# One DMA queue or two: loads from SyncE, stores from ScalarE, and other chunk sizes, in a softmax with a relative position bias

## The chip, the cores and the metric

The kernel runs on one core of a Trainium2 chip. Data lies in HBM, the large memory; the engines work on SBUF, a memory of 128 partitions (rows) on the core. DMA engines, 16 for the core, move data between the two. A transfer is issued by an engine's instruction queue (here that of SyncE, called SP, or that of ScalarE, called ACT), and the DMA engines then carry it out on their own. VectorE (DVE) and ScalarE compute; TensorE is not used.

The metric is the device time of one execution in microseconds (us). Before the change three runs gave 1330.45, 1329.27 and 1329.56, so the median is 1329.56 us.

## The reference

```python
B, H, S = (2, 8, 2112);  max_rel = 16
rel  = pos[:, None] - pos[None, :]
bias = rel_bias[:, np.clip(rel, -16, 16) + 16]          # (H, S, S)
logits = logits + bias[None]
logits = logits - logits.max(axis=-1, keepdims=True)
exp = np.exp(logits)
return exp / exp.sum(axis=-1, keepdims=True)
```

The input `logits` has 2 x 8 x 2112 x 2112 float32 values, 285.5 MB, and the output has as many. Each row of 2112 values gets a bias that depends only on the distance from the diagonal (33 different values per head), and then a softmax. Every value is read once and written once.

## The kernel before, in words

**Tiling.** Heads are taken in pairs, `K = H // 2 = 4` of them, and for each pair both batches, so there are 8 head pairs of matrices. The 128 partitions are 2 heads x 64 blocks, and a block is `W = 33` consecutive rows of a matrix. So partition p holds 33 rows of one head, contiguous in HBM. These 33 rows are cut into chunks: `SIZES = [6, 5, 6, 5, 6, 5]` (L35). A chunk of r rows is one transfer of 128 partitions x r rows x 8448 bytes, and it lies in one of `NBUF = 4` buffers `X[b]`, b = m % 4. `CH` (L39) lists the `NT = 12` chunks of one value of k (two batches of six), and a loop over k runs four times, so there are 48 chunks in all.

**The bias.** At the start of each k, `strip(k)` (L143) builds on VectorE a strip `F` of 2112 + 32 values per partition, such that the bias of row i of any block is a window of `F`, shifted by one for each row.

**A chunk's work.** `add(m)` (L169, VectorE) waits for the load, then for each row adds the bias, writes the negated sum and its minimum (L173). `exps(m)` (L178, ScalarE) follows row by row: the exponential and its sum (L181). `scale(m)` (L186, VectorE) waits for all of the chunk's exponentials, takes the reciprocals of the sums (L189), and multiplies the first `DV = 3` rows (L193); `scale_rest(m)` (L195) multiplies the other 2 or 3 rows on ScalarE (L198). VectorE starts on the next chunk's `add` only after its part of the scaling, so the chunks are computed one after the other.

**Order of transfers.** All loads and stores are issued by SyncE, on one queue (q1 of the profile), which is worked off in the order of issue. `load` (L86) issues the load of a chunk. `store` (L90) first waits for the scaled rows of VectorE (`scaled`) and of ScalarE (`scaledA`). The first four loads come first, then store 0, and then `turn` (L214) repeats: store chunk n, wait until store n - 1 has landed (its buffer is free), load chunk n + 3 into that buffer. The last chunk's store is cut in two, the 3 rows of VectorE and the 2 of ScalarE (L227, L228). `take(eng, sem, n)` (L82) is a wait for a semaphore to reach n, followed by taking n off it; each engine's loop over k (L202, L207, L221) is a real loop, so the counts must return to their start within a turn.

Of the kernel before, what the change touches and what calls it, by code (L numbers as in the profile page):

```python
# [11 lines left out]
ENG = mybir.EngineType  # L12
# [3 lines left out]
def kernel(  # L16
# [6 lines left out]
    nc = tc.nc  # L23
    P = 128
    B, H, S, S2 = logits.shape
    assert S == S2
    MR = 16
    W = 2 * MR + 1
    NB = S // W
    K = H // 2  # L30
# [1 line left out]
    FW = S + W - 1  # L32
    BIG = 3.0e38
    NBUF = 4
    SIZES = [6, 5, 6, 5, 6, 5]  # L35
    R = max(SIZES)
    assert sum(SIZES) == W

    CH = [(b, sum(SIZES[:i]), r) for b in range(B) for i, r in enumerate(SIZES)]  # L39
    NT = len(CH)  # L40
    assert NT % NBUF == 0

    io = ctx.enter_context(tc.tile_pool(name="io", bufs=1))
    X = [io.tile([P, R * S], FP32, tag=f"X{b}", name=f"X{b}") for b in range(NBUF)]
# [5 lines left out]
    tot = io.tile([P, NBUF * R], FP32, tag="tot", name="tot")  # L50
    rec = io.tile([P, NBUF * R], FP32, tag="rec", name="rec")
# [7 lines left out]
    def rows(t, k, m, s0, n):  # L59

        b, j, r = CH[m]
        return bass.AP(
            tensor=t.tensor,
            offset=t.offset + (b * H * S + j + s0) * S + k * (2 * S * S),
            ap=[[W * S, P], [1, n * S]],
        )

    with tc.tile_critical(no_gpsimd_drain=True):  # L68
        ld = [nc.alloc_semaphore(f"ld{b}") for b in range(NBUF)]
        st = [nc.alloc_semaphore(f"st{b}") for b in range(NBUF)]  # L70
        added = nc.alloc_semaphore("added")
        expd = nc.alloc_semaphore("expd")
        scaled = nc.alloc_semaphore("scaled")
        scaledA = nc.alloc_semaphore("scaledA")
        inv = nc.alloc_semaphore("inv")
        invA = nc.alloc_semaphore("invA")
        rb = nc.alloc_semaphore("rb")
        zero = nc.alloc_semaphore("zero")
        idx = nc.alloc_semaphore("idx")
        dve = nc.alloc_semaphore("dve")  # L80

        def take(eng, sem, n):  # L82
            eng.wait_ge(sem, n).then_inc(sem, -n)  # L83


        def load(k, m):  # L86
            b, r = m % NBUF, CH[m][2]
            nc.sync.dma_start(out=X[b][:, 0 : r * S], in_=rows(logits, k, m, 0, r)).then_inc(ld[b], 16)

        def store(k, m, s0=0, n=None):  # L90
            b, n = m % NBUF, n or CH[m][2]
            if s0 < DV:
                take(nc.sync, scaled, DV)
            if s0 + n > DV:
                take(nc.sync, scaledA, s0 + n - DV)
            nc.sync.dma_start(
                out=rows(out, k, m, s0, n), in_=X[b][:, s0 * S : (s0 + n) * S]
            ).then_inc(st[b], 16)

        for m in range(NBUF):  # L100
            load(0, m)

        Q = 32
        step = list(F.ap[0])[0]
        nc.vector.memset(F[:, 0 : H * W], 0.0).then_inc(zero, 1)  # L105
        nc.scalar.wait_ge(zero, 1)
        nc.scalar.dma_start(
            out=bass.AP(tensor=F.tensor, offset=F.offset, ap=[[Q * step, P // Q], [1, H * W]]),
            in_=bass.AP(tensor=rel_bias.tensor, offset=rel_bias.offset, ap=[[0, P // Q], [1, H * W]]),
        ).then_inc(rb, 16)  # L110
        for p0 in (0, NB):
            nc.gpsimd.iota(  # L112
                F[p0 : p0 + NB, H * W : H * W + NB], pattern=[[-1, NB]], base=0,
                channel_multiplier=1, allow_small_or_imprecise_dtypes=True,
            ).then_inc(idx, 1)

        v = nc.vector
        done = [0]

        def then(ins):  # L120
            done[0] += 1
            ins.then_inc(dve, 1)

        def settle():
            take(v, dve, done[0])
            done[0] = 0


        v.wait_ge(idx, 2)
        iq = F[:, H * W : H * W + NB]  # L130
        for m, op in ((eq, ALU.is_equal), (lt, ALU.is_gt), (gt, ALU.is_lt)):
            then(v.tensor_scalar(out=m, in0=iq, scalar1=0.0, scalar2=None, op0=op))  # L132
        v.wait_ge(rb, 16)
        then(v.stream_shuffle(out=F[:, 0 : H * W], in_=F[:, 0 : H * W], mask=[0] * Q))  # L134
        settle()
        for h in range(2):
            p = slice(h * NB, (h + 1) * NB)
            src = bass.AP(tensor=F.tensor, offset=F[p].offset + h * W,
                          ap=[[list(F.ap[0])[0], NB], [2 * W, K], [1, W]])
            then(v.tensor_copy(out=rbP[p], in_=src))  # L140
        settle()

        def strip(k):  # L143

            then(v.tensor_copy(out=rbK[:, :], in_=rbP[:, bass.ds(k, 1), :]))  # L145
            settle()
            low, high = rbK[:, W - 1 : W], rbK[:, 0:1]
            blocks = view(F, MR, [[W, NB], [1, W]])
            then(v.tensor_tensor(out=blocks, in0=view(eq, 0, [[1, NB], [0, W]]),  # L149
                                 in1=view(rbK, W - 1, [[0, NB], [-1, W]]), op=ALU.mult))  # L150
            then(v.tensor_scalar(out=rest, in0=lt, scalar1=low, scalar2=None, op0=ALU.mult))  # L151
            then(v.tensor_copy(out=F[:, 0:MR], in_=low.to_broadcast([P, MR])))  # L152
            then(v.tensor_copy(out=F[:, FW - MR : FW], in_=high.to_broadcast([P, MR])))  # L153
            settle()
            then(v.scalar_tensor_tensor(out=rest, in0=gt, scalar=high, in1=rest, op0=ALU.mult, op1=ALU.add))  # L155
            settle()
            then(v.tensor_tensor(out=blocks, in0=blocks, in1=view(rest, 0, [[1, NB], [0, W]]), op=ALU.add))  # L157
            settle()

        def row(m, i):  # L160
            return X[m % NBUF][:, i * S : (i + 1) * S]

        def col(t, m, i, n=1):
            c = m % NBUF * R + i
            return t[:, c : c + n]

        DV = 3

        def add(m):  # L169
            take(v, ld[m % NBUF], 16)  # L170
            j, r = CH[m][1:]
            for i in range(r):
                v.tensor_tensor_reduce(  # L173
                    out=row(m, i), in0=row(m, i), in1=F[:, W - 1 - j - i : W - 1 - j - i + S],
                    scale=-1.0, scalar=BIG, op0=ALU.add, op1=ALU.min, accum_out=col(nmax, m, i),
                ).then_inc(added, 1)

        def exps(m):  # L178
            for i in range(CH[m][2]):
                take(nc.scalar, added, 1)  # L180
                nc.scalar.activation(  # L181
                    out=row(m, i), in_=row(m, i), func=ACTF.Exp, scale=-1.0, bias=col(nmax, m, i),
                    accum_out=col(tot, m, i),
                ).then_inc(expd, 1)

        def scale(m):  # L186
            r = CH[m][2]
            take(v, expd, r)
            v.reciprocal(out=col(rec, m, 0, r), in_=col(tot, m, 0, r)).then_inc(inv, 1)  # L189
            v.wait_ge(inv, 1).then_inc(inv, -1)  # L190
            v.sem_inc(invA, 1)
            for i in range(DV):
                v.tensor_scalar_mul(out=row(m, i), in0=row(m, i), scalar1=col(rec, m, i)).then_inc(scaled, 1)  # L193

        def scale_rest(m):  # L195
            take(nc.scalar, invA, 1)
            for i in range(DV, CH[m][2]):
                nc.scalar.activation(  # L198
                    out=row(m, i), in_=row(m, i), func=ACTF.Copy, scale=col(rec, m, i),
                ).then_inc(scaledA, 1)  # L200

        with nc.Fori(0, K, 1, engines=[ENG.DVE]) as k:  # L202
            strip(k)
            for m in range(NT):
                add(m)
                scale(m)
        with nc.Fori(0, K, 1, engines=[ENG.Activation]):  # L207
            for m in range(NT):
                exps(m)
                scale_rest(m)  # L210

        def turn(k, first, stop):  # L214
            for n in range(first, stop):
                store(k + n // NT, n % NT)
                take(nc.sync, st[(n - 1) % NBUF], 16)
                load(k + (n + 3) // NT, (n + 3) % NT)

        store(0, 0)  # L220
        with nc.Fori(0, K - 1, 1, engines=[ENG.SP]) as k:  # L221
            turn(k, 1, NT + 1)
        turn(K - 1, 1, NT - 3)
        for m in range(NT - 3, NT - 1):
            store(K - 1, m)
        r = CH[NT - 1][2]
        store(K - 1, NT - 1, 0, DV)  # L227
        store(K - 1, NT - 1, DV, r - DV)  # L228
        for b in range(NBUF):
            take(nc.sync, st[b], 32 if b == (NT - 1) % NBUF else 16)  # L230


# [28 lines left out]
```

## Time and profile before

| what | value |
|---|---|
| median of the runs | 1329.56 us |
| profiled execution, its own time | 1329.3 us |
| its span (first to last recorded work) | 1327.5 us |
| VectorE busy | 819.7 us, 62% |
| ScalarE busy | 808.8 us, 61% |
| bytes read and written | 285.48 MB and 285.47 MB |
| rate over the span | 430 GB/s |
| the queue q1, share of the 16 DMA engines' time | 99.8% |

The span is what the profile records of the execution; 1.8 us of the profiled execution's own time lie outside it. The rate counts loads and stores together. A queue's share of 16 engines is the time that its packets took, summed, over 16 times the span. "SPq", "ACTq" and "DVEq" in the profile's rows are the instruction queues of SyncE, ScalarE and VectorE: a row that names one as the releaser tells that the wait instruction at that line held the engine. What such a wait waited for is read from the code; for `add` it is the load of the chunk.

### The profile page before, as it was taken

The page shows a single profiled execution, that of the slowest core. Times are in us where ns is not written, and L with a number is a line of the kernel's source. Part 1 is how long each engine was busy: PE and PEld are TensorE (multiplying, and loading weights), DVE is VectorE, ACT ScalarE, POOL GpSimd, SP SyncE. Part 2 cuts the span into 40 slices and gives each one's busy share as a digit, 9 for nine tenths or more (in the row PEclk, how much of TensorE's full clock was granted, in tenths as well). Part 3 has the DMA queues.
Part 4 walks back from the last instruction along what each step waited for, and adds up shares of the span by engine and source line. Part 5 has one row for each costly group of instructions (what it writes and reads, how often), then busy time and mean ns, then how long its engine had stood idle before and what let it go on. Part 6 is the DMA issues. An engine that isn't in the chain of part 4 may idle for free. (4 is left out here: it accounts for less than half of the span.)

```text
span 1327.5 us, 2383 instructions
## 1 busy us (share of the span) xinstructions
DVE 819.7 (62%) x756; ACT 808.8 (61%) x652; POOL 0.6 (0%) x6
## 2 busy tenths in 40 slices
DVE  6875665558655566556866466664686547665572
ACT  3885575655756557555676566764667646675472
POOL 0000000000000000000000000000000000000000
DMA  9999999999999999999999999999999999999998
GB/s 407 427 424 425 430 433 429 432 431 433 434 430 438 423 439 431 432 432 433 438 436 429 433 430 435 433 430 441 427 439 428 435 431 437 434 436 427 436 427 376
DMA packets 13981, 571.00 MB, mean 430 GB/s; under 512 B 1556, under 2 KB 1560, under 8 KB 1560
## 3 DMA queue, kind: packets, MB, share of 16 engines
q1 hardware_dynamic: 13968, 570.96, 99.8%
q14 instruction: 5, 0.04, 0.0%
q10 hardware_dynamic: 8, 0.00, 0.0%
HBM read 285.48 MB, written 285.47 MB: 430 GB/s over the span
## 5 line engine op out<-in xcount | busy, mean ns | idle before, releaser
L173 DVE CUSTOM_DVE_ANT_0 X<-X,F 128x2112 f32<-128x2112 f32 x264 | 605.5, 2354 | 346.8 <-DVEq L83 346.8
L181 ACT ACTIVATE X<-X,nmax 128x2112 f32<-128x2112 f32 x264 | 542.2, 2054 | 411.5 <-ACTq L83 385.7
L198 ACT ACTIVATE X<-X,rec 128x2112 f32<-128x2112 f32 x120 | 238.7, 2046 | 29.0 <-ACTq L83 29.0
L193 DVE TENSOR_SCALAR X<-X,rec 128x2112 f32<-128x2112 f32 x144 | 181.4, 1316 | 11.6 <-DVEq L190 11.6
L189 DVE RECIPROCAL rec<-tot 128x6 f32<-128x6 f32 (+1 forms) x48 | 9.1, 190 | 116.1 <-DVEq L83 116.1
L181 ACT ACTIVATION_READ_ACCUMULATOR X<-X,nmax 128x1 f32 x264 | 49.3, 187 | 0.0
L181 ACT ACT_TABLE_LOAD x4 | 5.1, 1283 | 55.8 <-ACTq L83 55.8
L173 DVE DVE_READ_ACCUMULATOR2_ANT nmax<- 128x1 f32 x264 | 21.7, 82 | 0.0
L157 DVE TENSOR_TENSOR F<-F,rest 128x2112 f32<-128x2112 f32 x4 | 9.4, 2358 | 0.6
L149 DVE TENSOR_TENSOR F<-Z,rbK 128x2112 f32<-128x2112 f32 x4 | 9.4, 2358 | 0.6
L134 DVE LOAD_MASK_SELECT F<-F x1 | 0.0, 14 | 7.1 <-DMA F<-in_rel_bias_dram 7.1
L155 DVE SCALAR_TENSOR_TENSOR rest<-Z,rbK,rest 128x64 f32<-128x64 f32 x4 | 1.1, 284 | 0.6 <-DVEq L83 0.2
L151 DVE TENSOR_SCALAR rest<-Z,rbK 128x64 f32<-128x64 f32 x4 | 1.1, 275 | 0.0
L105 DVE MEMSET F<- 128x264 f32 x1 | 0.3, 278 | 1.1 <-SPq L68 1.1
L145 DVE COPY rbK<-rbP 128x33 f32 x4 | 0.7, 178 | 0.3 <-DVEq L83 0.3
L153 DVE COPY F<-rbK 128x16 f32<-128x16 f32 x4 | 0.7, 168 | 0.0
L152 DVE COPY F<-rbK 128x16 f32<-128x16 f32 x4 | 0.7, 166 | 0.0
L132 DVE TENSOR_SCALAR Z<-F 128x64 f32<-128x64 f32 x3 | 0.5, 223 | 0.1
L140 DVE COPY rbP<-F 64x132 f32<-64x132 f32 x2 | 0.4, 224 | 0.2
L134 DVE STREAM_SHUFFLE F<-F 128x264 f32<-128x264 f32 x1 | 0.4, 443 | 0.0
L112 POOL IOTA F<- 64x64 f32 x2 | 0.4, 179 | 0.7 <-PEq L256 0.6
L245 POOL MEMSET const-bfloat16-1.0<- 128x1 bf16 x1 | 0.1, 103 | 0.0
(3 smaller groups left out, 0.3 us busy)
## 6 DMA issues: line engine op xcount, KB each, us to landing
X<-in_logits_dram SPq DMA_DIRECT2D x24, 6336.0 KB, 39.7
out_dram<-X SPq DMA_DIRECT2D x24, 6336.0 KB, 46.9
X<-in_logits_dram SPq DMA_DIRECT2D x24, 5280.0 KB, 42.2
out_dram<-X SPq DMA_DIRECT2D x23, 5280.0 KB, 48.6
out_dram<-X SPq DMA_DIRECT2D x1, 3168.0 KB, 16.5
out_dram<-X SPq DMA_DIRECT2D x1, 2112.0 KB, 21.1
F<-in_rel_bias_dram ACTq DMA_DIRECT2D x1, 4.1 KB
```

The lines of the kernel that those rows point to most:

```text
L145: then(v.tensor_copy(out=rbK[:, :], in_=rbP[:, bass.ds(k, 1), :]))
L149: then(v.tensor_tensor(out=blocks, in0=view(eq, 0, [[1, NB], [0, W]]), in1=view(rbK, W - 1, [[0, NB], [-1, W]]), op=ALU.mult))
L151: then(v.tensor_scalar(out=rest, in0=lt, scalar1=low, scalar2=None, op0=ALU.mult))
L152: then(v.tensor_copy(out=F[:, 0:MR], in_=low.to_broadcast([P, MR])))
L153: then(v.tensor_copy(out=F[:, FW - MR : FW], in_=high.to_broadcast([P, MR])))
L155: then(v.scalar_tensor_tensor(out=rest, in0=gt, scalar=high, in1=rest, op0=ALU.mult, op1=ALU.add))
L157: then(v.tensor_tensor(out=blocks, in0=blocks, in1=view(rest, 0, [[1, NB], [0, W]]), op=ALU.add))
L173: v.tensor_tensor_reduce(out=row(m, i), in0=row(m, i), in1=F[:, W - 1 - j - i : W - 1 - j - i + S], scale=-1.0, scalar=BIG, op0=ALU.add, o ...
L181: nc.scalar.activation(out=row(m, i), in_=row(m, i), func=ACTF.Exp, scale=-1.0, bias=col(nmax, m, i), accum_out=col(tot, m, i),).then_inc( ...
L189: v.reciprocal(out=col(rec, m, 0, r), in_=col(tot, m, 0, r)).then_inc(inv, 1)
L193: v.tensor_scalar_mul(out=row(m, i), in0=row(m, i), scalar1=col(rec, m, i)).then_inc(scaled, 1)
L198: nc.scalar.activation(out=row(m, i), in_=row(m, i), func=ACTF.Copy, scale=col(rec, m, i),).then_inc(scaledA, 1)
```

## The change

Four edits go together.

1. **Two queues.** `store` is now issued by ScalarE, at the end of each chunk's `scale_rest` in ScalarE's loop. SyncE issues the loads alone: `turn` waits for store n to land and then loads chunk n + 4 into the same buffer.
2. **Chunk sizes.** The first batch of a head pair is cut into 3, 6, 6, 6, 6, 6 rows and the second into 6, 6, 6, 6, 5, 4. There are still 12 chunks for each k and 48 in all. The last store is one transfer of 4 rows.
3. **Division of the scaling.** VectorE takes `r // 2` rows of a chunk of r (3 of 6, 2 of 5, 2 of 4, 1 of 3), ScalarE the rest. Before, VectorE took 3 always.
4. **Waits.** `scaledA` and `invA` are gone: both engines count on `scaled`, and both wait for a running count of `inv` that is put back at the last chunk of a turn. `exps` waits for `added` to reach i + 1 and takes the whole count off at the last row, instead of one at each row.

```diff
-    SIZES = [6, 5, 6, 5, 6, 5]
-    R = max(SIZES)
+    SIZES = [[3, 6, 6, 6, 6, 6], [6, 6, 6, 6, 5, 4]]
+    R = 6
...
-        def store(k, m, s0=0, n=None):
-            b, n = m % NBUF, n or CH[m][2]
-            if s0 < DV:
-                take(nc.sync, scaled, DV)
-            if s0 + n > DV:
-                take(nc.sync, scaledA, s0 + n - DV)
-            nc.sync.dma_start(
-                out=rows(out, k, m, s0, n), in_=X[b][:, s0 * S : (s0 + n) * S]
-            ).then_inc(st[b], 16)
+        def dv(m):
+            return CH[m][2] // 2
+
+        def store(k, m):
+            b, r = m % NBUF, CH[m][2]
+            take(nc.scalar, scaled, r)
+            nc.scalar.dma_start(out=rows(out, k, m, 0, r), in_=X[b][:, 0 : r * S]).then_inc(st[b], 16)
...
         def exps(m):
-            for i in range(CH[m][2]):
-                take(nc.scalar, added, 1)
+            r = CH[m][2]
+            for i in range(r):
+                if i < r - 1:
+                    nc.scalar.wait_ge(added, i + 1)
+                else:
+                    take(nc.scalar, added, r)
...
+        def scales_begin(eng, m):
+            if m < NT - 1:
+                eng.wait_ge(inv, m + 1)
+            else:
+                take(eng, inv, NT)
+
         def scale(m):
             r = CH[m][2]
             take(v, expd, r)
-            v.reciprocal(out=col(rec, m, 0, r), in_=col(tot, m, 0, r)).then_inc(inv, 1)
-            v.wait_ge(inv, 1).then_inc(inv, -1)
-            v.sem_inc(invA, 1)
-            for i in range(DV):
+            v.reciprocal(out=col(rec, m, 0, r), in_=col(tot, m, 0, r)).then_inc(inv, 1 if m < NT - 1 else NT + 1)
+            scales_begin(v, m)
+            for i in range(dv(m)):
...
         def scale_rest(m):
-            take(nc.scalar, invA, 1)
-            for i in range(DV, CH[m][2]):
+            scales_begin(nc.scalar, m)
+            for i in range(dv(m), CH[m][2]):
                 nc.scalar.activation(
                     out=row(m, i), in_=row(m, i), func=ACTF.Copy, scale=col(rec, m, i),
-                ).then_inc(scaledA, 1)
+                ).then_inc(scaled, 1)
...
             for m in range(NT):
                 exps(m)
                 scale_rest(m)
+                store(k, m)
...
         def turn(k, first, stop):
             for n in range(first, stop):
-                store(k + n // NT, n % NT)
-                take(nc.sync, st[(n - 1) % NBUF], 16)
-                load(k + (n + 3) // NT, (n + 3) % NT)
-
-        store(0, 0)
+                take(nc.sync, st[n % NBUF], 16)
+                load(k + (n + NBUF) // NT, (n + NBUF) % NT)
+
         with nc.Fori(0, K - 1, 1, engines=[ENG.SP]) as k:
-            turn(k, 1, NT + 1)
-        turn(K - 1, 1, NT - 3)
-        for m in range(NT - 3, NT - 1):
-            store(K - 1, m)
-        r = CH[NT - 1][2]
-        store(K - 1, NT - 1, 0, DV)
-        store(K - 1, NT - 1, DV, r - DV)
...
+            turn(k, 0, NT)
+        turn(K - 1, 0, NT - NBUF)
+        for m in range(NT - NBUF, NT):
+            take(nc.sync, st[m % NBUF], 16)
```

More of the change, by code (lines that the diff above doesn't have):

```diff
@@ L34 @@
     NBUF = 4
-    SIZES = [6, 5, 6, 5, 6, 5]
-    R = max(SIZES)
-    assert sum(SIZES) == W
-    CH = [(b, sum(SIZES[:i]), r) for b in range(B) for i, r in enumerate(SIZES)]
+    SIZES = [[3, 6, 6, 6, 6, 6], [6, 6, 6, 6, 5, 4]]
+    R = 6
+    assert all(sum(z) == W for z in SIZES) and len(SIZES) == B
+    CH = [(b, sum(SIZES[b][:i]), r) for b in range(B) for i, r in enumerate(SIZES[b])]
     NT = len(CH)
@@ L73 @@
         scaled = nc.alloc_semaphore("scaled")
-        scaledA = nc.alloc_semaphore("scaledA")
         inv = nc.alloc_semaphore("inv")
-        invA = nc.alloc_semaphore("invA")
         rb = nc.alloc_semaphore("rb")
@@ L165, in col @@
             return t[:, c : c + n]
-        DV = 3
         def add(m):
@@ L206 @@
                 scale(m)
-        with nc.Fori(0, K, 1, engines=[ENG.Activation]):
+        with nc.Fori(0, K, 1, engines=[ENG.Activation]) as k:
             for m in range(NT):
@@ L210 @@
                 scale_rest(m)
+                store(k, m)
         def turn(k, first, stop):
             for n in range(first, stop):
-                store(k + n // NT, n % NT)
-                take(nc.sync, st[(n - 1) % NBUF], 16)
-                load(k + (n + 3) // NT, (n + 3) % NT)
-        store(0, 0)
+                take(nc.sync, st[n % NBUF], 16)
+                load(k + (n + NBUF) // NT, (n + NBUF) % NT)
         with nc.Fori(0, K - 1, 1, engines=[ENG.SP]) as k:
-            turn(k, 1, NT + 1)
-        turn(K - 1, 1, NT - 3)
-        for m in range(NT - 3, NT - 1):
-            store(K - 1, m)
-        r = CH[NT - 1][2]
-        store(K - 1, NT - 1, 0, DV)
-        store(K - 1, NT - 1, DV, r - DV)
-        for b in range(NBUF):
-            take(nc.sync, st[b], 32 if b == (NT - 1) % NBUF else 16)
+            turn(k, 0, NT)
+        turn(K - 1, 0, NT - NBUF)
+        for m in range(NT - NBUF, NT):
+            take(nc.sync, st[m % NBUF], 16)
 _INS = ['logits', 'rel_bias']
```

## The prediction

> **What bounds the kernel now.** I read the head of the page first, then the queues, then the rate by stage, and last the timeline at both ends.
>
> ```profile
> span 1327.5 us, 2383 instructions
> DVE 819.7 (62%) x756; ACT 808.8 (61%) x652; POOL 0.6 (0%) x6
> DMA packets 13981, 571.00 MB, mean 430 GB/s; under 512 B 1556, under 2 KB 1560, under 8 KB 1560
> q1 hardware_dynamic: 13968, 570.96, 99.8%
> q14 instruction: 5, 0.04, 0.0%
> ```
>
> No computing engine is busy for more than 62%, but the one queue's packets fill 99.8% of the 16 DMA engines' time: the kernel is bound by its transfers. The bytes are fixed by the problem, so only the rate and the two ends can change.
>
> ```profile
> 0.00:60.00 60.00, 43.19 (x48) 34.82 (x29) 0.56 (x6) 1.00 0.98 410
> 60.00:400.00 340.00, 217.69 (x200) 216.84 (x177) 0.00 (x0) 1.00 1.00 431
> 400.00:1300.00 900.00, 554.82 (x506) 552.70 (x445) 0.00 (x0) 1.00 1.00 433
> 1300.00:1327.50 27.50, 3.97 (x4) 4.41 (x4) 0.00 (x0) 1.00 0.85 366
> 940.00:1160.00 220.00, 138.83 (x128) 135.69 (x110) 0.00 (x0) 1.00 1.00 434
> 720.00:940.00 220.00, 133.16 (x121) 134.71 (x109) 0.00 (x0) 1.00 1.00 432
> ```
>
> These are stretches of the span; the last two columns are the DMA engines' share and GB/s. In the middle 900 us the rate is 433. At it, 570.96 MB take 570.96 / 433 = 1318.6 us. What the span has above that sits in three places: 60 x (433 - 410) / 433 = 3.2 us at the start, 340 x (433 - 431) / 433 = 1.6 us up to 400 us, and 27.5 x (433 - 366) / 433 = 4.3 us at the end. The sum is 1327.7 us against a span of 1327.5, the profiled execution's own time is 1329.3 and the median 1329.56. I forecast against the median: the span plus 2.1 us. About 0.2% (2.7 us) is what a measurement of this kernel can tell from no change.
>
> **The change, part by part.**
>
> *The computing must stay under the transfers.* These rows are the size of a 6-row load, and then a 5-row chunk, a 6-row chunk and the start of the last chunk:
>
> ```profile
> X<-in_logits_dram SPq DMA_DIRECT2D x24, 6336.0 KB, 39.7
> 1231.62 2.36 DVE L173 CUSTOM_DVE_ANT_0 X<-X,F 128x2112 f32<-128x2112 f32 x1 [7.04 <-DVEq L83]
> 1245.98 4.00 ACT L198 ACTIVATE X<-X,rec 128x2112 f32<-128x2112 f32 x2 [0.60 <-ACTq L83]
> 1259.19 2.36 DVE L173 CUSTOM_DVE_ANT_0 X<-X,F 128x2112 f32<-128x2112 f32 x1 [9.47 <-DVEq L83]
> 1261.48 2.35 DVE L173 CUSTOM_DVE_ANT_0 X<-X,F 128x2112 f32<-128x2112 f32 x1
> 1275.80 3.78 DVE L193 TENSOR_SCALAR X<-X,rec 128x2112 f32<-128x2112 f32 x3 [0.24 <-DVEq L190]
> 1275.83 5.95 ACT L198 ACTIVATE X<-X,rec 128x2112 f32<-128x2112 f32 x3 [0.61 <-ACTq L83]
> 1286.66 2.36 DVE L173 CUSTOM_DVE_ANT_0 X<-X,F 128x2112 f32<-128x2112 f32 x1 [7.08 <-DVEq L83]
> ```
>
> A 6-row chunk takes 1275.83 + 5.95 - 1259.19 = 22.6 us from its first add to its last scaled row. Its load and store are 2 x 6336 KB = 12.98 MB, 30.0 us at 433 GB/s. So 7.4 us are free for each chunk, as the idle times in the brackets (7.04 to 9.47) say too. A 5-row chunk takes 18.4 us before; with one row moved from VectorE to ScalarE (5.95 - 4.00 = 1.95 us) it takes 20.3, against 25.0 of transfer. Chunks of 4 and 3 rows take one and two adds less than 18.4 (1261.48 - 1259.19 = 2.29 each): 16.1 and 13.8 us, against 20.0 and 15.0. All of it stays hidden, and the new division of the scaling costs nothing; the cover is the transfer time, and if it went, ScalarE's extra rows would cost 136 - 120 = 16 rows (17 of each 33 instead of 15, eight times) by 1.95 us, 31 us.
>
> *Issuing from ScalarE.*
>
> ```profile
> L96 SPq DMA_DIRECT2D out_dram<-X x49: 332/338/1001, 41.4 to 1305.3; - x49
> L88 SPq DMA_DIRECT2D X<-in_logits_dram x48: 339/349/512, 1.0 to 1244.0; - x48
> ACT X L181 <- ACTq L83: 385.7, 44, 12.5
> SPq L83 <- SPq L83: 1276.6, 141, 36.3
> ```
>
> A store's issue took SyncE 0.34 us (at most 1.0). ScalarE now spends that 48 times, 16 us and at most 48, inside 385.7 us of waiting for adds. Ahead of each store ScalarE gets a wait for `scaled`; queued behind it are the next chunk's exponentials, and VectorE's reciprocal waits for those. By the rows above VectorE's three scaled rows take 3.78 us and ScalarE's own three 5.95 from the same start, so the wait ends with ScalarE's own last row: it costs nothing but the issue. If the cover were gone, the price would be those 16 us. SyncE loses 49 issues and their waits; it waited for 1276.6 us, so that is worth nothing. The merged waits and the dropped `sem_inc` touch ScalarE's 0.6 us before its scaling and VectorE's 0.2, both hidden; nothing is expected of them.
>
> *The start.*
>
> ```profile
> 0.97 1.88 SPq L88 DMA_DIRECT2D X<-in_logits_dram  x4
> 14.10 2.36 DVE L157 TENSOR_TENSOR F<-F,rest 128x2112 f32<-128x2112 f32 x1
> 18.60 2.36 DVE L173 CUSTOM_DVE_ANT_0 X<-X,F 128x2112 f32<-128x2112 f32 x1 [2.15 <-DVEq L83]
> 41.38 16.61 SPq L96 DMA_DIRECT2D out_dram<-X  x2
> ```
>
> The 6-row first load of 15 us arrived for 18.60, so transfers begin near 2.3 us and a load is seen about 1.3 us after its end (an estimate from these rows). The 3-row load is there by 11, but the bias strip ends at 16.5, so chunk 0 is scaled at 16.5 + 13.8 = 30.3 and its store goes out some 11 us earlier than at 41.38. That buys nothing: 21 rows of loads keep the engines busy until 2.3 + 52.4 = 54.7, and the second chunk's store is ready by about 51. The 3.2 us stay.
>
> *The middle.* Both queues hold work: at equal shares a load and a store take 30 us each, so a buffer's round is 30 + 22.6 + 30 and some 3 us of landings, 85 of the 120 us that four chunks need. Loads are queued ahead all the time. What is unknown is the rate when each DMA engine has a load and a store to work on by turns. Before, the queue's 13968 packets belong to 49 + 48 = 97 transfers, 144 each; (13981 - 1560) / 97 = 128 of them are long, so an engine changes direction after 8 long packets, 96 times in all; at worst it will now change after each, some 670 times more. The nearest rows: the stretch at 432 differs from the one at 434 by 220 x 2 / 433 = 1.0 us in 16 transfers, 0.06 us a transfer; the whole 900 us fall short of 434 by 2.1 us in 65 transfers, 0.03 us each. If all of that were the price of a change of direction, 670 more cost 20 us (0.03) to 40 us (0.06). If none is, they cost nothing, and evenly mixed traffic may hold 434: 570.96 / 434 = 1315.6, so 3.0 us gained, and with the early 1.6 us 4.6. I take 0, nearest to the rows: both stretches of 220 us lie within 1 GB/s of 433 although each holds some 16 changes, so no price of them is seen.
>
> One rule bounds the gain. The Trainium skill, "DMA: Bandwidth & Descriptors", section "Issuing engines are not separate DMA queues", says that transfers from different engines interleave on the same 16 DMA engines, and that issuing from several saves the sequencer's issue time alone. By it two queues would be worth nothing here, as SyncE has 1276.6 us of waiting to spare; only a run with two queues can test it.
>
> *The end.* Before, the last store's last part was issued with SyncE's other stores:
>
> ```profile
> 1250.08 56.24 SPq L96 DMA_DIRECT2D out_dram<-X  x4
> 1301.02 4.00 ACT L198 ACTIVATE X<-X,rec 128x2112 f32<-128x2112 f32 x2 [0.60 <-ACTq L83]
> ```
>
> It was issued by 1306.3, while the last 5 rows' 12.5 us had to begin about 1314: a margin of 8 us. After, when the last load (4 rows) ends, its store is ready 1.3 + 16.1 + 1.4 (issue and first packet, as at the start) = 18.8 us later. Until then the engines have the 5-row store, 12.5 us, and what is left of the 6-row store before it, 0 to 15 us. At the middle that is 20.0 us: no gap, with about 1 us to spare; at the worst a gap of 6.3 us. I take 0 and keep both ends; a gap would be idle DMA just before the last store. The 4.3 us stay.
>
> The sum: 1318.6 + 3.2 + 1.6 + 4.3, as before; 1329.56 plus nothing, 1330 us.
>
> **The rivals.**
>
> *A change of direction has a price (slower).* Per-packet alternation costs each engine some 0.01 to 0.03 us: 670 changes give 7 to 20 us, so 1336 to 1350 us. For it: the first 400 us, with the same pattern, ran at 431, and 0.06 us a transfer lay between two stretches. Against it: 433 held over 900 us. It decides from 0.004 us a change, where it passes 2.7 us.
>
> *Evenly mixed traffic runs better (faster).* The early 1.6 us go and the rate holds 434: 1329.6 - 4.6 = 1325 us. For it: 434 is reached in one stretch. Against it: 99.8% of the engines' time is taken already, so only shorter packets can give it. The Trainium skill, same page, section "Where 436 GB/s comes from", gives a ceiling of 435.2 GB/s for all 16 ports; by that the gain could be 6.7 us, an estimate from that page, and the trace stays 0.5% under it.
>
> *The two directions overlap (much faster).* If a load and a store on one engine used separate paths, the rate would rise until computing bounds: 44 times 22.6 us (264 rows by 6) and some 31 us at the ends, about 1025 us. Nothing in the trace speaks for it: while one transfer ends and the next of the other direction begins, no stretch rises above 434.
>
> *The gap before the last store (slower)*, priced above: 0 to 6.3 us, with 3 us taken 1332.6.
>
> *Computing or instruction loading on the path (slower).* ScalarE's loop grows by 12 issues a turn; before, 5 instruction packets served all four turns. If each turn had to load code again behind full queues, 7 us of free time per chunk would still cover it. If not, some 5 us.
>
> **How the numbers follow.** No measurable change 0.33; price of direction 0.27; mixed traffic better 0.24; overlap 0.03; gap 0.10; code or computing 0.03. So faster 0.27, same 0.33, slower 0.40, and the time is that of the likeliest, 1330 us. The range goes from the rate of 434 with the early loss gone and a tidier end (some 4 of the 4.3 us), 1321 us, to the price at 0.03 us a change, 1350 us. It leaves out the overlap and the dearer changes of direction.
>
> **What would show it.** Two queues with about half of the packets each and together near 100% of 16 engines; 433 GB/s in the middle stretches; waits of VectorE for loads still there; ScalarE's wait before its stores short; the last store issued before the one ahead of it has ended. A middle rate under 432 means the price of direction, a rate over 434 one of the two faster rivals; a DMA share under 0.9 before the last store is the gap. If ScalarE's or VectorE's idle time went to nothing in the middle, the computing would be the bound, and the whole sum would be wrong.

## The result and the profile after

The changed kernel takes 1346.85 us in the median of five runs (1343.51 to 1348.55) against 1329.56 before: a ratio of 1.0127, 95% interval 1.0111 to 1.0143. It is slower by 17.3 us. The profiled execution took 1348.55 us, 1.8 us more than its span.

These are the head and the queues of the changed kernel's page; before, the one queue stood at 99.8%.

```profile
span 1346.8 us, 2037 instructions
DVE 800.1 (59%) x740; ACT 841.6 (62%) x668; POOL 0.6 (0%) x6
DMA packets 13837, 571.00 MB, mean 424 GB/s; under 512 B 1540, under 2 KB 1544, under 8 KB 1544
q1 hardware_dynamic: 6912, 285.48, 49.8%
q10 hardware_dynamic: 6920, 285.48, 49.1%
```

The bytes are the same and no engine is nearer to its limit. The queues now fill 98.9% of the DMA engines' time, over a longer span, and move 424 GB/s in place of 430. The stages of the changed kernel (last two columns: DMA share and GB/s) say where:

```profile
0.00:60.00 60.00, 45.77 (x50) 39.72 (x33) 0.56 (x6) 1.00 0.99 418
60.00:400.00 340.00, 200.86 (x185) 211.76 (x170) 0.00 (x0) 1.00 1.00 430
400.00:1300.00 900.00, 535.18 (x489) 566.02 (x449) 0.00 (x0) 1.00 1.00 429
1300.00:1346.80 46.80, 18.30 (x18) 24.08 (x19) 0.00 (x0) 1.00 0.67 290
```

Set against 433 GB/s as in the prediction, the stages fall short by 60 x 15 / 433 = 2.1 us, 340 x 3 / 433 = 2.4, 900 x 4 / 433 = 8.3 and 46.8 x 143 / 433 = 15.5. With 1318.6 that is 1346.9, the span. Before, the four terms were 3.2, 1.6, 0 and 4.3. So the middle lost 8.3 us and the end 11.2 us more; the start gained 1.1, the second stage lost 0.8.

**The middle: longer packets.** The DMA share there is 1.00, so the engines were not idle: their packets took longer. The trace holds each packet's own duration; a long packet (one partition's share of a transfer) took 1.87 us for 6 rows at its shortest, in every kernel here. The sum of all that long packets took above the shortest of their size, over 16 engines, is:

```
before  q1            12416 long packets,  291 more than 20 ns over, +5.4 us
after   q1 (loads)     6144 long packets,  509 more than 20 ns over, +11.7 us
after   q10 (stores)   6144 long packets,  136 more than 20 ns over, +1.5 us
```

It is the loads that got longer, by 0.37 us each where they did. Of these sums 1.5 us fell into the middle 900 us before and 9.4 us after (8.6 of them on loads): this accounts for 8.0 of the 8.3 us that the middle lost.

**The end: engines out of step.** Each engine's packets follow one another without a gap, so they can be strung into 16 rows (a reconstruction from start and end times). Up to 279 us eleven of the 16 engines had moved the same bytes, 4.190 MB of loads and 3.295 MB of stores; the hindmost had moved 0.236 MB less, 8.7 us at its 27.1 GB/s, and its own long packets above 0.15 us sum to 9.1 us. From then on single engines stayed 9 to 15 us behind: so much later than 90% of a load's packets did its last one end. A chunk's first add waits for the slowest engine's packets, so this delays the last chunks. Stretches of the changed kernel's end, and its timeline there (start and duration in us; in brackets how long VectorE had waited):

```profile
1305.00:1308.00 3.00, 1.93 (x3) 2.63 (x3) 0.00 (x0) 1.00 0.40 172
1308.00:1314.00 6.00, 0.81 (x1) 4.21 (x3) 0.00 (x0) 1.00 0.45 191
1314.00:1326.00 12.00, 8.24 (x7) 5.57 (x5) 0.00 (x0) 1.00 0.94 406
1326.00:1335.00 9.00, 3.70 (x5) 7.02 (x6) 0.00 (x0) 1.00 0.24 103
...
1286.68 0.34 ACTq L94 DMA_DIRECT2D out_dram<-X  x1
1292.14 2.36 DVE L167 CUSTOM_DVE_ANT_0 X<-X,F 128x2112 f32<-128x2112 f32 x1 [7.85 <-DVEq L81]
1312.43 0.34 ACTq L94 DMA_DIRECT2D out_dram<-X  x1
1317.76 2.36 DVE L167 CUSTOM_DVE_ANT_0 X<-X,F 128x2112 f32<-128x2112 f32 x1 [8.95 <-DVEq L81]
1333.91 0.34 ACTq L94 DMA_DIRECT2D out_dram<-X  x1
```

Of the last load's 128 long packets 90% had ended at 1301.8 us and the last at 1315.4; the load's last 4-byte packet, which marks its end, followed behind one more store packet at 1317.2, and the last chunk's first add starts at 1317.76. VectorE had waited 7.85 us for the load before and 8.95 us for this one. Most engines had nothing to do from about 1306 to the store issued at 1312.43, and again until the one issued at 1333.91. The store of 4 rows goes out 16.15 us after the first add, and some 13 us later the kernel ends.

### The profile page after: what moved, and what is told of

Read it like the earlier page. It is cut to its first block, busy times and chain, and to the rows that moved or that the text cites. A ratio compares the mean times of both kernels' runs of the same rounds, so it can differ in the third digit from the quotient of the medians.

```text
span 1346.8 us, 2037 instructions
## 1 busy us (share of the span) xinstructions
DVE 800.1 (59%) x740; ACT 841.6 (62%) x668; POOL 0.6 (0%) x6
## 5 line engine op out<-in xcount | busy, mean ns | idle before, releaser
L167 DVE CUSTOM_DVE_ANT_0 X<-X,F 128x2112 f32<-128x2112 f32 x264 | 605.5, 2354 | 404.6 <-DVEq L81 404.6
L179 ACT ACTIVATE X<-X,nmax 128x2112 f32<-128x2112 f32 x264 | 542.5, 2055 | 468.6 <-DVE nmax L167 435.8
L201 ACT ACTIVATE X<-X,rec 128x2112 f32<-128x2112 f32 x136 | 269.9, 2045 | 17.9 <-DVE rec L193 16.2
L196 DVE TENSOR_SCALAR X<-X,rec 128x2112 f32<-128x2112 f32 x128 | 161.7, 1316 | 2.1
L193 DVE RECIPROCAL rec<-tot 128x6 f32<-128x6 f32 (+3 forms) x48 | 9.1, 189 | 115.9 <-DVEq L81 115.9
```

Source lines behind the costliest of these rows:

```text
L167: v.tensor_tensor_reduce(out=row(m, i), in0=row(m, i), in1=F[:, W - 1 - j - i : W - 1 - j - i + S], scale=-1.0, scalar=BIG, op0=ALU.add, o ...
L179: nc.scalar.activation(out=row(m, i), in_=row(m, i), func=ACTF.Exp, scale=-1.0, bias=col(nmax, m, i), accum_out=col(tot, m, i),).then_inc( ...
L201: nc.scalar.activation(out=row(m, i), in_=row(m, i), func=ACTF.Copy, scale=col(rec, m, i),).then_inc(scaled, 1)
```

## The experiments

All times are medians of the runs; "before" stood at 1329.6 to 1330.1 us on the same chips. Two theories at the outset: A, two queues make the loads' packets longer, unevenly over the engines, and the hindmost engine holds up the end; B, the queues are free and the small last chunks make the gap at the end.

**1. Old chunk sizes, two queues.**

```diff
-    SIZES = [[3, 6, 6, 6, 6, 6], [6, 6, 6, 6, 5, 4]]
+    SIZES = [[6, 5, 6, 5, 6, 5], [6, 5, 6, 5, 6, 5]]
```

> The changed kernel with the chunk sizes of before (6, 5, 6, 5, 6, 5 in both batches); queues, waits and division of the scaling as changed. Theory A (two queues make the long packets of the loads longer, on some DMA engines more than on others, and the engines that fall behind hold up the end): the cost stays, 1338 to 1350 us, the load queue's packets again above 1.87 us per 6 rows, and DMA share below 0.75 in the last 45 us. Theory B (the chunk sizes make the gap at the end, and the queues cost nothing): back within 3 us of 1329.6.

Measured: 1334.68 us, ratio 1.0043 (1.0016 to 1.0070), and a spread that before does not have: ten executions from 1327.8 to 1344.45, where before keeps within 1328.66 to 1330.89. The profiled execution was the fastest, and it holds the middle:

```profile
400.00:1300.00 900.00, 536.10 (x490) 584.26 (x460) 0.00 (x0) 1.00 1.00 434
1300.00:1326.00 26.00, 3.05 (x5) 8.30 (x7) 0.00 (x0) 1.00 0.80 344
```

Neither theory is met. Two queues can run as well as one, but do so only in some executions, and the chunk sizes make up the larger part of the loss.

**2. New chunk sizes, one queue.** Merged waits and division of the scaling as changed; transfers on SyncE in the order of before.

```diff
-            take(nc.scalar, scaled, r)
-            nc.scalar.dma_start(out=rows(out, k, m, 0, r), ...)
+            take(nc.sync, scaled, r)
+            nc.sync.dma_start(out=rows(out, k, m, 0, r), ...)
...
-                take(nc.sync, st[n % NBUF], 16)
-                load(k + (n + NBUF) // NT, (n + NBUF) % NT)
+                store(k + n // NT, n % NT)
+                take(nc.sync, st[(n - 1) % NBUF], 16)
+                load(k + (n + 3) // NT, (n + 3) % NT)
```

> The changed kernel's chunk sizes, merged waits and division of the scaling, with all transfers on SyncE's one queue in the order of before (store n, then load n + 3); the last store in one piece. Theory A: 1327 to 1332 us, rate of 433 in the middle, as before. Theory B: 1337 us or more, since the small last chunks would leave the gap here too.

Measured: 1330.11 us, ratio 1.0003 (0.9994 to 1.0013). Chunk sizes, merged waits and the division of the scaling are worth nothing as long as one queue carries all. B falls. So the loss comes from two queues and the new sizes together.

**3 and 4. The transfers alone, on one queue and on two.** Computing is left out: 48 loads go into two buffers and 48 stores take zeros from two others, each waiting only for the landing of the one before the last of its own kind.

```diff
+            b, r = m % 2, CH[m][2]
+            nc.sync.dma_start(out=X[b][:, 0 : r * S], in_=rows(logits, k, m, 0, r)).then_inc(ld[b], 16)
...
+            eng.dma_start(out=rows(out, k, m, 0, r), in_=X[2 + b][:, 0 : r * S]).then_inc(st[b], 16)
```

> No computing: 48 loads of 6 and 5 rows into two buffers and 48 stores of zeros from two others, in turn on SyncE's queue, so the output holds zeros. Both theories: 1322 to 1328 us, 433 GB/s all along, little idle time at the end.

> The same transfers without computing, loads on SyncE's queue and stores on ScalarE's, neither waiting for the other; the output holds zeros. Theory A: 8 to 20 us slower than the one-queue stream, 425 to 431 GB/s in the middle, the loads' packets longer. Theory B: within 3 us of the one-queue stream. If only the waits between the two queues make the engines fall out of step, the middle stays at 433 and the end is ragged by less than 3 us.

Measured: 1328.92 us on one queue (0.9 us above the expected range), ratio to before 0.9995 (0.9985 to 1.0004); 1530.87 us on two. The middle of the first stream and then of the second:

```profile
400.00:1300.00 900.00, 0.00 (x0) 0.00 (x0) 1.00 1.00 433
...
400.00:1300.00 900.00, 0.00 (x0) 0.00 (x0) 1.00 0.99 377
```

The kernel before takes as long as its transfers alone on one queue. The second stream loses 202 us where A expected 8 to 20: 377 GB/s with the engines at 0.99, and 4655 of its 6144 long store packets more than 20 ns over the shortest, 118.5 us by 16 engines, besides 63.6 us on the loads. The stores started at 27.5 us, when two chunks had been loaded, and stayed two chunks behind. Two explanations were to be told apart: P, the rows that are read and written at one time; M, two full queues of opposite direction cost this much.

**5. The same two streams, stores at the rows that are being loaded.**

```diff
-            eng.dma_start(out=rows(out, k, m, 0, r), in_=X[2 + b]...)
+            eng.dma_start(out=rows(out, k, (m + 2) % NT, 0, r), in_=X[2 + b]...)
```

> The two-queue stream with the stores' place in HBM moved two chunks on, so that loads and stores are at the same rows of their tensors at the same time (before, the stores were two chunks behind); nothing else changes, and the output holds zeros. Theory P (the price hangs on which rows are read and written together): the 377 GB/s of the stream changes by over 10 GB/s, up or down, so the time leaves 1500 to 1560 us. Theory M (two full queues of opposite direction cost this much whatever they address): 1520 to 1540 us again.

Measured: 1531.09 us, and packets as long as in run 4 to within 1 us by 16 engines. For this shift of two chunks the rows do not matter.

**6. The same two streams, stores started later.** A third fill with zeros goes ahead of them, so that the first store is issued at 40.84 us in place of 27.52.

```diff
+        nc.vector.wait_ge(zero, 2)
+        nc.vector.memset(X[3][:, :], 0.0).then_inc(zero, 1)
...
-        nc.scalar.wait_ge(zero, 2)
+        nc.scalar.wait_ge(zero, 3)
```

> The two-queue stream with the stores started about 13 us later (a third fill of a buffer with zeros goes ahead of them), so that they stay about 2.9 chunks behind the loads in place of 2.0; output zeros. Theory P: faster by 50 us or more than the stream with two chunks, towards 1340 us, since the two-queue kernel that computes ran at 433 GB/s with its stores 2.6 chunks behind. Theory M: 1530 to 1550 us.

Measured: 1330.03 us (1327.96 to 1336.10), ratio 1.0001 (0.9987 to 1.0016). 200 us are gone. In the middle of this kernel:

```profile
400.00:1300.00 900.00, 0.00 (x0) 0.00 (x0) 1.00 1.00 433
```

M falls: two queues of opposite direction run at 433. P's number was met, but run 5 had taken its ground away: the rows were moved there with no effect, and here only the time between the streams was. By the same reconstruction an engine of this stream changes queue some 600 to 630 times, and its load packets that lie between two store packets take 6 ns above the shortest on average. So a change of direction costs next to nothing.

**7 and 8. The new sizes in one batch only.**

```diff
-    SIZES = [[3, 6, 6, 6, 6, 6], [6, 6, 6, 6, 5, 4]]
+    SIZES = [[3, 6, 6, 6, 6, 6], [6, 5, 6, 5, 6, 5]]
```

```diff
-    SIZES = [[3, 6, 6, 6, 6, 6], [6, 6, 6, 6, 5, 4]]
+    SIZES = [[6, 5, 6, 5, 6, 5], [6, 6, 6, 6, 5, 4]]
```

> The changed kernel with the new sizes in the first batch alone (3, 6, 6, 6, 6, 6) and the old ones in the second. Theory T (the small last chunks 5, 4 leave the DMA engines idle before the last two stores): 1333 to 1338 us, as with the old chunks throughout. Theory L (unequal chunks put single DMA engines out of step with the others, wherever they stand): 1340 to 1348 us.

> The changed kernel with the new sizes in the second batch alone (6, 6, 6, 6, 5, 4) and the old ones in the first. Theory T: 1341 to 1348 us, since the end is that of the changed kernel. Theory L: between the old chunks' 1335 and 1347, as for the first batch alone.

Measured: 1343.04 us (1341.40 to 1346.39), ratio 1.0094 (1.0077 to 1.0111), with the new first batch; 1338.68 us (1329.39 to 1342.51), ratio 1.0068 (1.0050 to 1.0086), with the new second. The first batch's sizes alone bring most of the loss although the end is that of before. The ends, of run 7 and then of run 8's profiled execution, its fastest:

```profile
1300.00:1344.60 44.60, 16.32 (x15) 20.95 (x16) 0.00 (x0) 1.00 0.66 286
...
1300.00:1327.60 27.60, 8.21 (x9) 11.27 (x10) 0.00 (x0) 1.00 0.83 356
```

With the old last chunks the end is as ragged as the changed kernel's (0.66 of the engines' time against 0.67), and with the new ones, in an execution of 1329.39 us, it is not. T falls: the last chunks' sizes do not make the gap. What goes with it in these two executions is the engines' being out of step: the last load's hindmost packet ended 11.9 us after 90% of them in run 7's, 4.6 us in run 8's. L holds for the first batch; the second alone does less.

**9. Of the change, only the queues and the merged waits.** Run 1 with VectorE's 3 rows of each chunk.

```diff
-            return CH[m][2] // 2
+            return 3
```

> Two queues with the chunk sizes and the division of the scaling of before (VectorE 3 rows of each chunk): of the change only the queues and the merged waits are left. Theory S (out of step: in some executions a DMA engine falls behind the others early, its packets stay long, and it holds up the end; the division has no part): a spread of 1328 to 1344 us as with the old chunks alone, median 1331 to 1338, and where the profiled execution is a slow one, one or two engines end their loads 8 us or more after the others. Theory D (the division of the scaling delays the stores): 1328 to 1331 in all executions.

Measured: 1338.11 us, twelve executions from 1327.77 to 1342.37, ratio 1.0049 (1.0026 to 1.0072). D falls, and S's spread is there: three executions at 1327.8 to 1328.7, nine at 1336.5 to 1342.4. The profiled one is one of the nine: 1339.4 us, a middle of 430, long load packets +9.4 us (in run 1's profile, of 1327.8 us: +3.4), but its last load's hindmost packet ended only 3.3 us after 90% of them. The 8 us that S expected there were not met, and yet the end falls short by 37.7 x (433 - 317) / 433 = 10.1 us, against 4.3 before. So an engine far behind is not the only thing that opens a gap at the end; what did it here was not found.

```profile
400.00:1300.00 900.00, 551.03 (x504) 552.75 (x445) 0.00 (x0) 1.00 1.00 430
1300.00:1337.70 37.70, 15.45 (x14) 14.74 (x12) 0.00 (x0) 1.00 0.73 317
```

**10. The short chunk last in its batch.**

```diff
-    SIZES = [[3, 6, 6, 6, 6, 6], [6, 6, 6, 6, 5, 4]]
+    SIZES = [[6, 6, 6, 6, 6, 3], [6, 6, 6, 6, 5, 4]]
```

> The changed kernel with the 3-row chunk as the last of the first batch in place of the first (6, 6, 6, 6, 6, 3 and 6, 6, 6, 6, 5, 4). Theory F (the first, short store going out at 30 us amid the first loads puts an engine out of step from the start): 1331 to 1340 us with a wide spread, as with the new second batch alone. Theory U (chunks of unequal size put engines out of step at any time): 1342 to 1349 us as the changed kernel.

Measured: 1378.56 us, six executions from 1345.61 to 1390.08, ratio 1.0369 (1.0323 to 1.0415). F falls by every execution, the fastest too: without a short first store the kernel is no faster. U's range holds the fastest, 1345.61 us, alone; its middle is 428. The other five lie between 1368.96 and 1390.08, up to 41 us above U's range, and none of them was profiled, so it is open in which stage they lost it.

**11. The two streams, stores about 2.4 chunks behind.** Run 6 with half of the third fill; the first store is issued at 34.24 us.

```diff
-        nc.vector.memset(X[3][:, :], 0.0).then_inc(zero, 1)
+        nc.vector.memset(X[3][:, 0 : 3 * S], 0.0).then_inc(zero, 1)
```

> The two-queue stream with the stores started about 5 us later than in the first one, so that they stay about 2.4 chunks behind; output zeros. Theory W (only stores a whole number of chunks behind collide with the loads): 1328 to 1340 us. Theory G (the nearer the stores are to two chunks behind, the more): between 1345 and 1500 us.

Measured: 1332.44 us (1325.58 to 1335.99), ratio 1.0011 (0.9994 to 1.0028), the middle at 433. W's number is met and G falls: 2.4 chunks behind is as good as 2.9, and two whole chunks cost 200 us. Whether other whole numbers of chunks would cost as much wasn't tried.

**12. The same streams, with the changed kernel's chunk sizes.** Run 11 with the new `SIZES`, and no other edit.

```diff
-    SIZES = [6, 5, 6, 5, 6, 5]
+    SIZES = [[3, 6, 6, 6, 6, 6], [6, 6, 6, 6, 5, 4]]
```

> The two-queue stream with the stores some 13 rows behind the loads, as in the run before it, but with the changed kernel's chunk sizes (3, 6, 6, 6, 6, 6 and 6, 6, 6, 6, 5, 4); output zeros. Theory E (runs of chunks of equal size let a load's packets and a store's fall into a pattern that makes them long): 1340 us or more, the packets longer in the middle, without any computing. Theory C (only together with the waits for computed chunks do the sizes cost time): 1326 to 1336 us, as with chunks of 6 and 5.

Measured: 1344.66 us (1342.23 to 1347.13), ratio 1.0104 (1.0087 to 1.0120).

```profile
400.00:1300.00 900.00, 0.00 (x0) 0.00 (x0) 1.00 1.00 429
1300.00:1345.40 45.40, 0.00 (x0) 0.00 (x0) 1.00 0.69 297
```

E's number is met and C falls. Without any computing, two queues with these sizes show the changed kernel's 429 in the middle, its ragged end (0.69, 297) and its time within 2.2 us. Their long packets in the middle sum to 9.4 us above the shortest, as in the changed kernel; in run 11 to 1.4. The stores stayed some 16 rows behind the loads for most of the run, and not 13 as expected, but so they did in run 6 with the old sizes (15 to 16), at 433. So the loss is one of the transfers: two queues, with chunks of these sizes.

What the sizes do to the packets was not shown. E's reason, that loads and stores of equal size meet at an engine, does not hold by itself. In run 11 some 60% of the load packets between two store packets have the stores' size, and they are 3 ns over the shortest on average; in run 12 those of equal size are 17 ns over and the others 25 (from the reconstructed rows). And run 9 has no two equal chunks in a row, and still nine of its twelve executions lost time.

## Why the prediction was right and wrong

The time lies in the range, and slower was the likeliest sign (0.40). The forecast, no measurable change at 1330 us, was wrong by 17 us. That the range holds the time is in good part luck: its upper end was the price of changes of direction, which proved to be next to nothing, and the loss came from longer load packets and from engines out of step, which no term of the sum had.

**What bounds it, the start, the computing: right.** The kernel is bound by transfers, and run 3 shows that before sat on the floor of one queue. The start's 3.2 us became 2.1. Computing stayed hidden: VectorE still waits 404.6 us for loads, ScalarE 435.8 us for adds, and the last chunk took 16.15 us from its first add to its store's issue, against 16.1 foreseen.

```profile
DVE X L167 <- DVEq L81: 404.6, 47, 16.5
ACT X L179 <- DVE nmax L167: 435.8, 47, 16.2
L94 ACTq DMA_DIRECT2D out_dram<-X x48: 338/338/383, 29.4 to 1333.9; - x48
```

**Issuing from ScalarE, waits, sizes, division, each costed at nothing: right as long as one queue carries all.** A store's issue takes 0.34 us on ScalarE too, and run 2 has all the rest at 1330.11. But the sizes were costed on one queue's ground. That they could matter to two queues, by the packets, was not thought of; it is worth 1346.85 - 1334.68 = 12 us.

**The middle, "I take 0, nearest to the rows": wrong**, by 8.3 us. The rows came from a single queue, and no row of it could show what two do. The rival gave 7 to 20 us and has the size, but not the mechanism: per change of direction the price is nothing. The streams of runs 6 and 11 change queue some 600 to 640 times an engine and hold 433. (The 96 changes that the prediction counted before are 89 by the code's order, since the first four loads, the first two stores and the last stores follow one another; this changes nothing of the argument.) What the runs show in its place: load packets that got longer, 9.4 us by 16 engines in the middle against 1.5, by an amount that hangs on chunk sizes and on the time between loads and stores; at worst (run 4) it was 182 us over the whole kernel.

**The end, "no gap, with about 1 us to spare": wrong**, by 11.2 us. The working let a transfer land at once on all engines. At the last load the hindmost engine was 13.6 us behind 90% of the packets, so the last chunks' computing began late and most engines ran dry twice, before 1312.43 and before 1333.91. The worst case named, 6.3 us, knew one gap, and rested on the small last chunks, without which run 7's end is as ragged.

**The faster rivals: not met.** No kernel with two queues had a middle above 434, so the two directions do not overlap. The best execution of the kernels that compute, 1327.77 us, is 1.8 us under before's median; the streams reached 1325.58. By the rule of the Trainium skill, "DMA: Bandwidth & Descriptors", section "Issuing engines are not separate DMA queues", a second queue gains nothing; the runs agree (1330.03 us on two queues in run 6, 1328.92 on one in run 3). That interleaving on the same engines may also cost, as in runs 4 and 12, the rule does not say, and there the measurement goes further. The ceiling of 435.2 GB/s in the Trainium skill, "DMA: Bandwidth & Descriptors", section "Where 436 GB/s comes from", was not passed either: the middle 900 us of every kernel here ran at 434 or less.

## What to carry to other kernels

When one queue already fills the DMA engines, as here (99.8%), a second one has little to give and may cost (here 5 to 17 us in the median with the sizes of the two kernels): time the bare transfers on one queue first, and if the kernel is within its spread of that, leave the transfers alone. Cost every part of a change on the ground that the other parts make, here chunk sizes on two queues. With loads and stores on two queues, look at several executions and not at one, since the same kernel ran at 1328 and at 1342 us.

## What was not expected of the hardware

- Two streams of opposite direction on two queues ran at 377 GB/s or at 433, and which of them was decided by starting the stores 6.7 us later (34.24 us against 27.52). Moving the stores' rows in HBM by two chunks made no difference. Why is open: the time between the streams also sets which partitions of SBUF are read and written at one time, and no run tells that apart.
- Engines fall out of step and stay so: single ones 9 to 15 us behind from 279 us on in the changed kernel. On one queue the stream's engines also ended up to 6.7 us apart (1320.7 to 1327.4 us), without its middle falling below 433.
- The spread of executions can tell of such trouble, though not always: 2.2 us with one queue before, 14.6 us in run 9 and 44.5 us in run 10, but only 5.0 us in the changed kernel, which lost time in every execution.
